# One plain feed-forward chunk instead of two, and two chunk pairs opened early

## Chip, cores, metric

The kernel runs on one core of a Trainium2 chip. The metric is the device time of one execution in microseconds (us): before the change a median of 2859.53 us over 3 runs (2858.35 to 2859.78). "Before" is the kernel as it was; line numbers L... are those of its profile unless said otherwise.

## What is computed

A trunk of two layers over 768 tokens (512 of one request, 256 of another), width 1024. Each layer is a feed-forward block, a mixer, and a second feed-forward block, so there are four feed-forward blocks, f0 to f3. The mixers (a gated linear recurrence between f0 and f1, windowed attention between f2 and f3) are not touched. What is:

```python
x = x + 0.5 * swiglu_ffn(rmsnorm(x, norm_g[li, 0]), ffn_w1[li, 0], ffn_w2[li, 0])

def swiglu_ffn(x, w1, w2):                    # D_FF = 2816
    gate, up = jnp.split(x @ w1, 2, axis=-1)
    return (jax.nn.silu(gate) * up) @ w2
```

The hidden width 2816 is 22 chunks of 128 columns; a chunk has 128 gate columns and 128 up columns.

## The kernel before

**Number format.** All products of float32 operands are made of three TensorE matmuls on "hi" and "lo" halves: hi·hi, hi·lo, lo·hi. Each operand is split once: ScalarE (ACT) casts it to hi, VectorE (DVE) subtracts to get lo (`split`, L265 to L267 for activations; L166/L167 and L199/L200 for weights).

**A plain chunk** (`up_plain`, L398) multiplies 8 blocks of input columns (k) by the gate and the up weights, for one half of the tokens (384) at a time: 2 × 8 × 3 = 48 matmuls of 384 columns per token half, 96 for both.

**A pair** (`up_pair`, L431) treats a chunk's gate and up weights as a 2 × 2 matrix product over (two halves of the input width) × (two halves of the tokens) and does it with 7 products instead of 8 (Strassen's scheme in Winograd's form): 7 × 4 × 3 = 84 matmuls of 384 columns. The products take these operands (`FACTOR`, L45): p1 takes b00 and p2 takes b10, the two input halves of token half 0; p3 takes b11; p4, p5, p6, p7 take t4, t1, t2, t3. The t's are differences of the b's of **both** token halves, formed by `sums`/`mix` (L348 to L362): four subtractions and four splits of 768 elements per partition, for each of two k-halves (kp 0 and 1), on DVE and ACT. One product is 12 matmuls, 6 for each kp; the first of each three needs only the hi parts.

**A feed-forward block** (`ffn`, L503): 5 groups of 4 chunks, each group followed by its share of the second matrix (`down_quad`, L458, matmuls at L479), and 2 last chunks. Chunks 0 and 1 (`PLAIN = 2`) are plain, and are worked token half by token half: chunk 0 half 0, chunk 1 half 0, chunk 0 half 1, chunk 1 half 1. Chunks 2 to 21 are pairs. While chunks 0 and 1 run for token half 0, the rest of the preparation of token half 1 is taken in at set points (`run_later`, L406): normalised token blocks (`norm_block`, L300; scaling L306) are transposed by TensorE (`turn`, L323), copied and split; then `sums` makes the t's. In f1 to f3 the sixth token block gets its norm only as the preceding stage ends.

**Weights.** `load_next` (L143) loads a chunk's gate and up weights into raw tiles (`wr`, 4 buffers) through SP's queue; GpSimd (POOL) adds one raw half into another by accumulating DMAs (L141) for a pair. A list of steps then turns raw tiles into split tiles (`w`, at most 8 units held at once, `WBUFS`); `ahead` (L244) takes the next step whenever a product has released its tile. For pairs these steps include two in-place sums on DVE (L206 after p1, L210 after p2). p5's lo part is made on POOL, the others on DVE (L200).

A scheduler in the framework orders the recorded instructions on each engine; each engine then executes its list strictly in order.

Of the kernel before, what the change touches and what calls it, by code (L numbers as in the profile page):

```python
# [12 lines left out]
AF = mybir.ActivationFunctionType  # L13
# [3 lines left out]
P = 128  # L17
# [28 lines left out]


class Trunk:
# [83 lines left out]
        self.nc.scalar.dma_start(self.band, self.consts[3])  # L132

    def plan(self, key, src, shape):
        self.queue.append((key, (src,), shape, None))

    def plan_quad(self, key, srcs, shape, order):
        self.queue.append((key, srcs, shape, order))

    def into(self, out, src):  # L140
        self.nc.gpsimd.dma_start(out, src, accum_op=ALU.add)  # L141

    def load_next(self):  # L143
        key, srcs, shape, how = self.queue.pop(0)
        raws = []
        for src in srcs:
            t = self.wp.tile([P, 1024], F32, tag="wr", name=self.name("wr"), bufs=RAWBUFS)
            raw = t[:, : shape[0] * shape[1]].rearrange("p (a b) -> p a b", a=shape[0])
            if len(srcs) < 4:
                src = src.rearrange("(k p) c -> p k c", p=P)  # L150
# [6 lines left out]
        self.loaded.append((len(raws), steps))  # L157

    def wtile(self):
        return self.wp.tile([P, 1024], F32R, tag="w", name=self.name("w"), bufs=WBUFS)  # L160
# [11 lines left out]
    def quad_steps(self, key, raws, srcs, order):  # L172
        nc = self.nc
        flat = lambda t: t.rearrange("p a b -> p (a b)")
        up = len(raws) == 2
        if up:
            a11, a12, a21, a22 = (flat(t[:, h : h + 4, :]) for t in raws for h in (0, 4))
            three = [srcs[1].rearrange("(k p) c -> p k c", p=P)[:, :4, :]]
        else:
            a11, a12, a21, a22 = (flat(t) for t in raws)  # L180
            three = [srcs[2][:, i : i + 1, :] for i in range(2)]
        s3 = []
        for i, src in enumerate(three):
            t = self.wp.tile([P, 512], F32, tag="s3", name=self.name("s3"), bufs=2)
            self.last_load = nc.sync.dma_start(t.rearrange("p (a b) -> p a b", a=src.shape[1]), src)
            self.into(t, a11[:, i * 512 : (i + 1) * 512])
            s3.append(t)
        self.into(a21, a22)

        def split(name, srcs, eng=None):  # L190
            if up:
                w = self.wtile()
                hi, lo = w[:, :512], w[:, 512:]
            else:
                hi, lo = self.wtile(), self.wtile()
            n = srcs[0].shape[-1]
            for i, src in enumerate(srcs):
                h, l = (t[:, i * n : (i + 1) * n] for t in (hi, lo))
                nc.scalar.copy(h, src)  # L199
                (eng or nc.vector).tensor_sub(l, src, h.bitcast(F32))  # L200
            view = lambda t: t.rearrange("p (a b) -> p a b", a=4 if up else 2)
            self.staged[(*key, name)] = (view(hi), view(lo), 1 if up else 2)

        def p1():
            split("p1", [a11])
            nc.vector.tensor_add(a11, a11, a21)  # L206
# [14 lines left out]
        return [(1 if up else 2, steps[name]) for name in order]  # L221

    def stage_next(self):
        if not self.loaded:
            self.load_next()
        steps = self.loaded[0][1]
        n, go = steps.pop(0)
        go()
        self.held += n
        if not steps:  # L230
            self.loaded.pop(0)
        while self.queue and sum(e[0] for e in self.loaded) + len(self.queue[0][1]) <= RAWBUFS:
            self.load_next()

    def take(self, key):
# [142 lines left out]
    def plan_ffn(self, tag, w1, w2):  # L378
        def up(i):
            gate, up = (w1[:, c * P : (c + 1) * P] for c in (i, NF + i))  # L380
            if i < PLAIN:
                self.plan((tag, i, 0), gate, (NC, P))
                self.plan((tag, i, 1), up, (NC, P))
            else:
                self.plan_quad((tag, i), (gate, up), (NC, P), UP)

        for g in range(GROUPS):
            for i in range(4 * g, 4 * g + 4):
                up(i)
# [8 lines left out]
    def up_plain(self, tag, j, half):  # L398
        pss = []
        for c in range(2):  # L400
            wh, wl = self.take((tag, j, c))
            ps = self.ps(H)
            for k in range(NC):
                b = self.operand(f"b{k // 4}{half}", k % 4)
                self.mm3(ps, (wh[:, k, :], wl[:, k, :]), b, k == 0, k == NC - 1)
                if half == 0 and k in (((), (2, 6)), ((3, 7), (3, 7)))[j][c]:  # L406
                    self.run_later()
            if half:
                self.done((tag, j, c))
# [18 lines left out]
                )  # L428
        self.done((*key, name))

    def up_pair(self, tag, j):  # L431
        nc = self.nc
        key = (tag, j)
        a, b, c, d = (self.ps(H) for _ in range(4))
        v, w, t = (self.tmp(H) for _ in range(3))
        p = lambda name, ps, first, last: self.product(key, name, FACTOR[name], ps, first, last)
        p("p1", a, True, False)
        nc.scalar.copy(v, a)
        p("p7", c, True, False)
        nc.scalar.copy(w, c)  # L440
        p("p2", a, False, True)
        nc.scalar.activation(a, a, AF.Silu)
        p("p5", d, True, False)
        nc.vector.tensor_sub(w, w, d)  # L444
        p("p4", c, False, True)
# [57 lines left out]
    def ffn(self, tag, next_row):  # L503
        for g in range(GROUPS):
# [7 lines left out]
            def gather(ts, kp):  # L512
                self.mix(ts[0], ts[1], ts[2], ts[3], lambda name, src: put(name, src, kp))

            if g == 0:
# [766 lines left out]
```

## Time and profile before

| | |
|---|---|
| runs shown | 2859.53 us median (2858.35 to 2859.78) |
| the profiled execution's own time | 2859.59 us |
| its span in the trace | 2857.8 us |
| TensorE busy | 2804.0 us (98%) |
| VectorE busy | 2175.1 us (76%) |
| ScalarE busy | 1317.9 us (46%) |
| mean granted TensorE clock | 0.997 |

The span is what the trace covers; the execution's own time is 1.8 us longer. A busy time is the union of the instructions' intervals on an engine. TensorE's matmuls overlap (each is shown with some 334 ns for 384 columns, and starts 173 ns after the one before), so lost time on TensorE is read from the "idle before" column and from distances between starts.

### The profile page before, as it was taken

The page shows a single profiled execution, that of the slowest core. Times are in us where ns is not written, and L with a number is a line of the kernel's source. Part 1 is how long each engine was busy: PE and PEld are TensorE (multiplying, and loading weights), DVE is VectorE, ACT ScalarE, POOL GpSimd, SP SyncE. Part 2 cuts the span into 40 slices and gives each one's busy share as a digit, 9 for nine tenths or more (in the row PEclk, how much of TensorE's full clock was granted, in tenths as well). Part 3 has the DMA queues.
Part 4 walks back from the last instruction along what each step waited for, and adds up shares of the span by engine and source line. Part 5 has one row for each costly group of instructions (what it writes and reads, how often), then busy time and mean ns, then how long its engine had stood idle before and what let it go on. Part 6 is the DMA issues. An engine that isn't in the chain of part 4 may idle for free. (4 is left out here: it accounts for less than half of the span.)

```text
span 2857.8 us, 40567 instructions
## 1 busy us (share of the span) xinstructions
PE 2804.0 (98%) x15225; PEld 2556.4 (89%) x15225; DVE 2175.1 (76%) x3750; ACT 1317.9 (46%) x2454; POOL 358.4 (13%) x402
## 2 busy tenths in 40 slices
PE   8999999999999999999999999999999999999998
PEld 8889999889899889998998998999887779989997
DVE  7788787477577658878878877887847868778877
ACT  7344443434344435434444543444457755434443
POOL 1111111000000001111111111111002211111110
PEclk9999999999999999999999999999999999999999
DMA  6554454311111133554444355444412113554443
GB/s 164 127 124 122 117 136 120 111 45 38 45 41 35 61 94 89 133 129 122 122 115 111 89 134 130 121 122 119 125 67 75 37 46 91 135 129 122 118 122 96
DMA packets 330102, 291.37 MB, mean 102 GB/s; under 512 B 11609, under 2 KB 257841, under 8 KB 329905
## 3 DMA queue, kind: packets, MB, share of 16 engines
q1 hardware_dynamic: 294064, 212.43, 25.2%
q0 software_dynamic: 31680, 62.93, 12.6%
q10 hardware_dynamic: 4160, 13.42, 1.3%
q8 instruction: 119, 1.95, 0.3%
q14 instruction: 79, 0.64, 0.1%
HBM read 216.39 MB, written 9.44 MB: 79 GB/s over the span
## 5 line engine op out<-in xcount | busy, mean ns | idle before, releaser
L421 PE MATMUL ps<-big,w 128*128 128x384 f32 x6720 | 1173.1, 334 | 3.1 <-DVE tA L444 3.0
L421 PEld LDWEIGHTS ps<-big,w 128*128 128x128 f32 x6720 | 1165.4, 188 | 9.0 <-DVE tA L444 7.3
L199 ACT CAST w<-wr 128x512 fp32r<-128x512 f32 x600 | 415.9, 707 | 722.6 <-PE ps L421 320.6
L479 PE MATMUL ps<-w,big 128*128 128x512 f32 x2520 | 586.5, 391 | 17.9 <-DVE x L501 17.8
L479 PEld LDWEIGHTS ps<-w,big 128*128 128x128 f32 x2520 | 469.6, 188 | 129.8 <-DVE x L501 17.4
L200 DVE TENSOR_TENSOR w<-wr,w 128x512 fp32r<-128x512 f32 (+1 forms) x520 | 438.9, 854 | 94.7 <-ACT w L199 86.1
L501 DVE SCALAR_TENSOR_TENSOR x<-ps,x 128x512 f32<-128x512 f32 x468 | 305.8, 683 | 20.8 <-PE ps L479 10.4
L141 POOL DMA_DIRECT2D s<-wr x120 | 105.6, 880 | 1333.9 <-DMA wr<-in_ffn_w_dram 590.5
L261 PE MATMUL ps<-w,big 128*128 128x512 f32 x624 | 249.9, 401 | 0.2
L263 PE MATMUL ps<-w,big 128*128 128x512 f32 x624 | 245.3, 393 | 1.3 <-DVE big L330 1.3
L262 PE MATMUL ps<-w,big 128*128 128x512 f32 x624 | 244.8, 392 | 0.0
L266 ACT CAST big<-tA 128x384 fp32r<-128x384 f32 x296 | 147.9, 512 | 175.6 <-DVE tA L449 72.4
L261 PE MATMUL ps<-big,w 128*128 128x384 f32 (+2 forms) x640 | 221.6, 347 | 2.1 <-ACT big L266 2.0
L262 PE MATMUL ps<-big,w 128*128 128x384 f32 (+2 forms) x640 | 217.4, 340 | 0.6 <-DVE big L267 0.5
L263 PE MATMUL ps<-big,w 128*128 128x384 f32 (+2 forms) x640 | 216.3, 338 | 0.0
L167 DVE TENSOR_TENSOR w<-wr,w 128x1024 fp32r<-128x1024 f32 x92 | 111.8, 1223 | 81.7 <-ACT w L166 57.7
L141 POOL DMA_DIRECT2D wr<-wr x100 | 87.2, 872 | 682.5 <-DVE tA L350 317.9
L267 DVE TENSOR_TENSOR big<-tA,big 128x384 fp32r<-128x384 f32 x296 | 164.2, 566 | 8.0 <-ACT big L266 4.6
L206 DVE TENSOR_TENSOR wr<-wr,wr 128x512 f32<-128x512 f32 (+1 forms) x100 | 79.4, 794 | 114.8 <-DMA wr<-wr 85.0
L166 ACT CAST w<-wr 128x1024 fp32r<-128x1024 f32 x92 | 96.6, 1052 | 122.2 <-PE ps L262 101.1
L263 PEld LDWEIGHTS ps<-w,big 128*128 128x128 f32 x624 | 117.7, 189 | 27.0 <-DVE big L330 2.0
L200 POOL TENSOR_TENSOR w<-wr,w 128x512 fp32r<-128x512 f32 x80 | 118.6, 1482 | 158.4 <-ACT w L199 145.3
(170 smaller groups left out, 3327.5 us busy)
## 6 DMA issues: line engine op xcount, KB each, us to landing
wr<-in_ffn_w_dram SPq DMA_DIRECT2D x264, 512.0 KB, 3.9
s<-in_ffn_w_dram SPq DMA_DIRECT2D x120, 256.0 KB, 3.0
s<-wr POOLq DMA_DIRECT2D x120, 256.0 KB, 3.8
wr<-wr POOLq DMA_DIRECT2D x80, 256.0 KB, 3.9
wr<-in_hg_w_in_dram SPq DMA_DIRECT2D x40, 512.0 KB, 3.8
wr<-wr POOLq DMA_DIRECT2D x20, 512.0 KB, 4.6
spill<-x ACTq DMA_DIRECT2D x12, 512.0 KB, 3.1
x<-spill ACTq DMA_DIRECT2D x12, 512.0 KB, 3.3
```

The costliest lines, as they stand in the source:

```text
L141: self.nc.gpsimd.dma_start(out, src, accum_op=ALU.add)
L167: self.nc.vector.tensor_sub(lo, raw, hi.bitcast(F32))
L199: nc.scalar.copy(h, src)
L200: (eng or nc.vector).tensor_sub(l, src, h.bitcast(F32))
L261: nc.tensor.matmul(out, a[0], b[0], start=first, stop=False)
L262: nc.tensor.matmul(out, a[0], b[1], start=False, stop=False)
L263: nc.tensor.matmul(out, a[1], b[0], start=False, stop=last)
L266: self.nc.scalar.copy(hi, src)
L267: self.nc.vector.tensor_sub(lo, src, hi.bitcast(F32))
L421: self.nc.tensor.matmul(ps, a[x], b[y], start=first and k == 0 and i == 0, stop=k == 3 and i == 2, skip_group_check=True,)
L479: nc.tensor.matmul(ps, a[x], w[y], start=name == chain and kp == 0 and q == 0, stop=kp == 1 and q == 2, skip_group_check=True,)
L501: self.nc.vector.scalar_tensor_tensor(x, ps, c, x, ALU.mult, ALU.add)
```

## The change

- `PLAIN = 1`: only chunk 0 is plain. Chunk 1 becomes a pair; the number of groups stays 5 and of last chunks 2.
- In each block the order becomes: chunk 0 half 0; then `open_pairs` does p1 of chunks 1 and 2 and p2 of chunks 1 and 2 (with the copy and the SiLU that follow them); then chunk 0 half 1; then the five other products of chunk 1, those of chunk 2, and chunk 3 as a whole pair. The points of `run_later` move with it: two within chunk 0, one behind each of the four opened products.
- The weights of chunks 1 and 2 are planned as one entry of four raw tiles; their steps come as p1, p1, p2, p2, then the rest of chunk 1, then of chunk 2 (`OPENED`).
- For the two opened pairs p5's lo part is made on DVE instead of POOL.

```diff
-PLAIN = 2
+PLAIN = 1
+EARLY = 2
 UP = ("p1", "p7", "p2", "p5", "p4", "p6", "p3")
+OPENED = ("p1", "p2", "p7", "p5", "p4", "p6", "p3")
...
     def load_next(self):
-        key, srcs, shape, how = self.queue.pop(0)
+        lists, count = [], 0
+        for part in self.queue.pop(0):
+            steps, n = self.load_part(*part)
+            lists.append(steps)
+            count += n
+        if len(lists) > 1:
+            opened = [steps.pop(0) for _ in range(EARLY) for steps in lists]
+            lists.insert(0, opened)
+        self.loaded.append((count, sum(lists, [])))
...
-            "p5": lambda: split("p5", [a21], nc.gpsimd if up else None),
+            "p5": lambda: split("p5", [a21], nc.gpsimd if order == UP else None),
...
+            elif i < PLAIN + 2:
+                two.append(((tag, i), (gate, up), (NC, P), OPENED))
+                if len(two) == 2:
+                    self.queue.append(two)
...
-                if half == 0 and k in (((), (2, 6)), ((3, 7), (3, 7)))[j][c]:
+                if half == 0 and k in ((), (2, 6))[c]:
                     self.run_later()
...
+    def open_pairs(self, tag, js):
+        nc = self.nc
+        opened = {j: (self.ps(H), self.tmp(H)) for j in js}
+        for j, (a, v) in opened.items():
+            self.product((tag, j), "p1", FACTOR["p1"], a, True, False)
+            nc.scalar.copy(v, a)
+            self.run_later()
+        for j, (a, _) in opened.items():
+            self.product((tag, j), "p2", FACTOR["p2"], a, False, True)
+            nc.scalar.activation(a, a, AF.Silu)
+            self.run_later()
+        return opened
...
-                ts = {}
-                for half in range(2):
-                    for j in range(PLAIN):
-                        t = ts[2 * j + half] = self.up_plain(tag, j, half)
-                        name = f"b{j}{half}"
-                        if name != "b01":
-                            put(name, t, 0)
-                gather(ts, 0)
+                plain = [self.up_plain(tag, 0, 0)]
+                put("b00", plain[0], 0)
+                opened = self.open_pairs(tag, range(PLAIN, PLAIN + EARLY))
                 self.run_later(len(self.deferred))
+                plain.append(self.up_plain(tag, 0, 1))
             for kp in range(2):
-                if g == 0 and kp == 0:
-                    continue
                 ts = []
                 for j in range(2):
-                    for half, t in enumerate(self.up_pair(tag, 4 * g + 2 * kp + j)):
+                    i = 4 * g + 2 * kp + j
+                    if i < PLAIN:
+                        ts += plain
+                        continue
+                    for half, t in enumerate(self.up_pair(tag, i, opened.get(i))):
```

**What it moves on the engines.** Compared row by row, the instruction lists of before and after differ only at the start and in the first group of each of the four blocks. The second block, f1, is shown. In the rows, `w` are split weights, `wr` raw weights, `ps` accumulators in PSUM, `big` activations; the line numbers of the changed kernel are a little higher (L200 is L212 there, L306 is L318, L421 is L438).

TensorE in f1 before, at the end of the plain chunks (L261 to L263 are their three matmuls; the last plain accumulator is ps_9343) and at the start of chunk 2, the first pair (L421): p1 (b00), p7 (t3: big_9180 for kp 0, big_9196 for kp 1), p2 (b10), p5 (t1: big_9172, big_9188):

```order
L261 MATMUL ps_9343<-big_9145,w_9001 128x384
L262 MATMUL ps_9343<-big_9145,w_9001 128x384
L263 MATMUL ps_9343<-big_9145,w_9002 128x384
L421 MATMUL ps_9397<-big_8978,w_9270 128x384 x6
L421 MATMUL ps_9397<-big_8981,w_9270 128x384 x6
L421 MATMUL ps_9399<-big_9180,w_9274 128x384 x6
L421 MATMUL ps_9399<-big_9196,w_9274 128x384 x6
L421 MATMUL ps_9397<-big_9041,w_9302 128x384 x6
L421 MATMUL ps_9397<-big_9044,w_9302 128x384 x6
L421 MATMUL ps_9400<-big_9172,w_9306 128x384 x6
L421 MATMUL ps_9400<-big_9188,w_9306 128x384 x6
```

TensorE at the same place after the change: the end of chunk 0 (L273 to L275) is followed at once by the products of chunk 1 that need the t's (t3: big_9206 for kp 0, big_9222 for kp 1; t1: big_9198, big_9214; t2: big_9209, big_9225; t4: big_9203, big_9219):

```order
L274 MATMUL ps_9307<-big_9164,w_8855 128x384
L275 MATMUL ps_9307<-big_9164,w_8856 128x384
L438 MATMUL ps_9342<-big_9206,w_9192 128x384 x6
L438 MATMUL ps_9343<-big_9198,w_9240 128x384 x6
L438 MATMUL ps_9343<-big_9214,w_9240 128x384 x5
L438 MATMUL ps_9342<-big_9222,w_9192 128x384
L438 MATMUL ps_9343<-big_9214,w_9240 128x384
L438 MATMUL ps_9341<-big_9209,w_9272 128x384 x6
L438 MATMUL ps_9342<-big_9222,w_9192 128x384 x5
L438 MATMUL ps_9341<-big_9225,w_9272 128x384 x4
L438 MATMUL ps_9342<-big_9203,w_9256 128x384 x6
```

The products that need no t have moved ahead of this place, so that the first use of a t follows the plain matmuls directly, and the scheduler has interleaved the products of kp 0 with each other.

VectorE in f1 before, from the split of the first operands of token half 0 on (big_8978), past the weights of chunk 1 (L167), to the norm of the sixth token block (L306, big_9014):

```order
L267 TENSOR_TENSOR big_8978<-big_8961,big_8978 128x2x384
L267 TENSOR_TENSOR big_8981<-big_8961,big_8981 128x2x384
L167 TENSOR_TENSOR w_8992<-wr_8742,w_8991 128x1024
L465 TENSOR_TENSOR x_8537<-x_8537,x_8543 128x512
L167 TENSOR_TENSOR w_9002<-wr_8754,w_9001 128x1024
L305 RECIPROCAL stat_9015<-stat_9015 128x1
L306 TENSOR_SCALAR big_9014<-x_8543,stat_9015 128x1024
```

VectorE at the same place after the change, from the second of these splits to the norm of the sixth token block (L318, big_9033):

```order
L279 TENSOR_TENSOR big_9000<-big_8980,big_9000 128x2x384
L212 TENSOR_TENSOR w_9010<-wr_8859,w_9010 128x512
L212 TENSOR_TENSOR w_9014<-wr_8867,w_9014 128x512
L218 TENSOR_TENSOR wr_8859<-wr_8859,wr_8861 128x512
L218 TENSOR_TENSOR wr_8867<-wr_8867,wr_8869 128x512
L212 TENSOR_TENSOR w_9024<-wr_8859,w_9024 128x512
L212 TENSOR_TENSOR w_9028<-wr_8867,w_9028 128x512
L222 TENSOR_TENSOR wr_8859<-wr_8859 128x512
L222 TENSOR_TENSOR wr_8867<-wr_8867 128x512
L317 RECIPROCAL stat_9034<-stat_9034 128x1
L279 TENSOR_TENSOR big_9060<-big_9043,big_9060 128x2x384
L318 TENSOR_SCALAR big_9033<-x_8558,stat_9034 128x1024
```

Eight weight instructions of 512 (four splits, four sums) and one activation split now stand ahead of that norm, where two weight splits of 1024 and one update of x stood; the update of x has moved behind it.

More of the change, by code (lines that the diff above doesn't have):

```diff
@@ L134, in plan, with plan_quad @@
     def plan(self, key, src, shape):
-        self.queue.append((key, (src,), shape, None))
-    def plan_quad(self, key, srcs, shape, order):
-        self.queue.append((key, srcs, shape, order))
+        self.queue.append([(key, (src,), shape, None)])
+    def plan_quad(self, *args):
+        self.queue.append([args])
     def into(self, out, src):
@@ L231, in stage_next @@
             self.loaded.pop(0)
-        while self.queue and sum(e[0] for e in self.loaded) + len(self.queue[0][1]) <= RAWBUFS:
+        while self.queue and sum(e[0] for e in self.loaded) + sum(len(p[1]) for p in self.queue[0]) <= RAWBUFS:
             self.load_next()
@@ L429, in product, with up_pair @@
         self.done((*key, name))
-    def up_pair(self, tag, j):
+    def open_pairs(self, tag, js):
[10 more added lines that the diff above has]
+        return opened
+    def up_pair(self, tag, j, opened=None):
         nc = self.nc
         key = (tag, j)
-        a, b, c, d = (self.ps(H) for _ in range(4))
-        v, w, t = (self.tmp(H) for _ in range(3))
+        a, v = opened or (self.ps(H), self.tmp(H))
+        b, c, d = (self.ps(H) for _ in range(3))
+        w, t = (self.tmp(H) for _ in range(2))
         p = lambda name, ps, first, last: self.product(key, name, FACTOR[name], ps, first, last)
-        p("p1", a, True, False)
-        nc.scalar.copy(v, a)
+        if not opened:
+            p("p1", a, True, False)
+            nc.scalar.copy(v, a)
         p("p7", c, True, False)
         nc.scalar.copy(w, c)
-        p("p2", a, False, True)
-        nc.scalar.activation(a, a, AF.Silu)
+        if not opened:
+            p("p2", a, False, True)
+            nc.scalar.activation(a, a, AF.Silu)
         p("p5", d, True, False)
```

5 lines of the change are left out of this document (4 added, 1 removed).

## The prediction

> **What bounds the kernel now.** The page's first part, then TensorE's waits (line that waited, what ended the wait, us in all, times, longest):
>
> ```profile
> span 2857.8 us, 40567 instructions
> PE 2804.0 (98%) x15225; PEld 2556.4 (89%) x15225; DVE 2175.1 (76%) x3750; ACT 1317.9 (46%) x2454; POOL 358.4 (13%) x402
> PE ps L479 <- DVE x L501: 17.8, 37, 0.6
> PE ps L421 <- DVE tA L444: 3.0, 8, 0.7
> PE ps L261 <- ACT big L266: 2.0, 1, 2.0
> PE ps L323 <- DVE big L306: 1.9, 2, 1.2
> ```
>
> TensorE is busy 98% of the span and waits nowhere for long, so its instruction count is the time: fewer matmuls shorten the kernel, unless new waits take the place. The waits above lie in the second products (L479), at a group's last pair (L444) and at the program's start. The change touches the starts of the four blocks, so next I read the engines' busy time in these four stretches, from the first plain matmul to the last (columns: length, then busy time and instruction count of PE, PEld, DVE, ACT, POOL, then clock and DMA):
>
> ```profile
> 14.33:55.58 41.25, 39.72 (x216) 38.65 (x217) 35.29 (x46) 32.74 (x54) 5.54 (x5) 0.92 0.52 127
> 1069.79:1106.40 36.61, 36.52 (x219) 35.87 (x218) 32.64 (x42) 26.84 (x45) 3.88 (x3) 1.00 0.21 52
> 1569.12:1605.80 36.68, 36.63 (x219) 35.99 (x218) 33.23 (x44) 26.79 (x45) 4.49 (x3) 1.00 0.22 53
> 2353.90:2390.71 36.81, 36.61 (x219) 35.86 (x218) 32.84 (x42) 27.01 (x45) 3.88 (x3) 1.00 0.22 52
> ```
>
> TensorE loses nothing there, but DVE is busy 32.6 of 36.6 us: it works nearly as long as TensorE in just the stretch that is to be shortened. That decides this case.
>
> **What the change removes.** In each block a plain chunk (96 matmuls) becomes a pair (84): 12 matmuls of 384 columns fewer. Their pitch, from TensorE's list in f1 (start, length, count; the next group's start ends it):
>
> ```profile
> 1106.42 29.28 PE L421 MATMUL ps<-big,w 128*128 128x384 f32 x168
> 1135.54 4.88 PE L479 MATMUL ps<-w,big 128*128 128x512 f32 x19
> ```
>
> (1135.54 − 1106.42) / 168 = 0.1733 us, so 12 matmuls are 2.08 us and four blocks 8.3 us. That is all there is to gain: 2859.6 − 8.3 = 2851.3 us. [...]
>
> The first use of a t comes sooner. In f1 it stood 12 matmuls behind 1106.42; now it follows the plain matmuls, 48 matmuls (8.3 us) before 1106.42. The work that makes the t's does not shrink.
>
> **First wait: the sixth token block.** DVE's list in f1 (start, length, op, count, idle before):
>
> ```profile
> 1069.60 1.82 DVE L267 TENSOR_TENSOR big<-big,big 128x768 fp32r<-128x768 f32 x2
> 1071.34 1.22 DVE L167 TENSOR_TENSOR w<-wr,w 128x1024 fp32r<-128x1024 f32 x1
> 1072.47 0.69 DVE L465 TENSOR_TENSOR x<-x,x 128x512 f32<-128x512 f32 x1
> 1073.07 1.22 DVE L167 TENSOR_TENSOR w<-wr,w 128x1024 fp32r<-128x1024 f32 x1
> 1074.21 0.16 DVE L305 RECIPROCAL stat<-stat 128x1 f32<-128x1 f32 x1
> 1074.40 0.75 DVE L306 TENSOR_SCALAR big<-x,stat 128x1024 f32<-128x1024 f32 x1
> ...
> 1079.21 1.83 DVE L267 TENSOR_TENSOR big<-big,big 128x768 fp32r<-128x768 f32 x2 [1.53 <-ACT big L266]
> 1082.60 1.83 DVE L267 TENSOR_TENSOR big<-big,big 128x768 fp32r<-128x768 f32 x2 [1.56 <-ACT big L266]
> ```
>
> By distances between starts a 512-wide op takes 0.60 us (1072.47 to 1073.07) and a 768-wide one 0.87. After the change, from 1069.60: two splits 1.74, eight weight instructions 8 × 0.60 = 4.80, the reciprocal 0.2, one more split 0.87, the norm 0.75: the sixth block is ready at 1077.96, where before it was at 1075.15. TensorE's side:
>
> ```profile
> 1074.01 0.93 PE L323 MATMUL ps<-ident_r,big 128*128 128x128 f32 x7
> 1074.69 0.42 PE L261 MATMUL ps<-big,w 128*128 128x384 f32 x1
> ...
> 1075.30 0.71 PE L323 MATMUL ps<-ident_r,big 128*128 128x128 f32 x5
> ```
>
> Its transposes began at 1075.30 without a wait. Their new place is 8 plain matmuls (1.39 us) and 4 transposes (0.68/7 = 0.10 each) later, 1077.08. So TensorE waits some **1.0 us**; f3 has the same rows, f2 about 0.8. Bounds: 0, if DVE gets to the weights before 1069.60, and 2.8 us, the whole delay of the norm. I take 1.0, f1's value. The eight instructions need weights that POOL's accumulating DMAs have finished; those loads start when chunk 0's raw tiles come free, as chunk 2's did before, so I put no DMA wait there.
>
> **Second wait: the t's.** The transposes end about 1.8 us later than before, and ACT, then DVE follow. The [1.53] and [1.56] above show that DVE itself waited for ACT at this place, so most of its added work fits in, and not all of the delay adds up. The sums' first and last rows before:
>
> ```profile
> 1084.34 0.95 DVE L350 TENSOR_TENSOR big<-big,big 128x768 f32<-128x768 f32 x1
> ...
> 1099.05 2.69 DVE L267 TENSOR_TENSOR big<-big,big 128x768 fp32r<-128x768 f32 x3
> ```
>
> After: sums from 1086.1 on. Up to the lo part of t3 for kp 1 stand 15 ops of 768 (13.0), 5 of 512 (3.0) and 2 of 384 (0.9): 1103.1. TensorE starts the t products at 1106.42 − 8.32 + 1.0 = 1099.1 and reaches the first matmul that needs this lo part 25 matmuls later, at 1103.4; t2's lo part comes 0.9 later (1104.0) and is needed 30 matmuls in (1104.3). So there is **no wait, with 0.3 us to spare**; bounds −0.3 (hidden) and +3, if the two DVE gaps of 1.5 us persist in full. p4 follows only 4 matmuls (0.7 us) behind p7's end, with ACT's copy between them (some 0.5 us and two semaphores): 0.2 us.
>
> **Third wait: the last pair of the group.** Chunk 3's raw tiles come free only when chunk 1's last weight is split (1101 by the same count), and those of the second products when chunk 3's are. Before:
>
> ```profile
> 1130.05 1.23 DVE L206 TENSOR_TENSOR wr<-wr,wr 128x1024 f32<-128x1024 f32 x1 [5.17 <-DMA wr<-wr]
> 1131.19 1.22 DVE L200 TENSOR_TENSOR w<-wr,w 128x1024 fp32r<-128x1024 f32 x1
> 1132.33 0.55 DVE L444 TENSOR_TENSOR tA<-tA,ps 128x384 f32<-128x384 f32 x1
> ```
>
> The sum at 1130.05 waits for the accumulating DMA, and L444, which TensorE's p3 needs, stands behind it; that is the wait of 3.0 us in 8 places quoted above. After, by my count of DVE's rows, the raw tiles come free 1.5 us later and L444's successor ends near 1133.0, where TensorE wants it at 1132.6: 0.4 us (bounds 0 and 0.7, the longest of those 8). POOL no longer makes p5's lo part for two chunks; DVE's two extra splits are in the counts.
>
> f1 to f3, each: −2.08 + 1.0 + 0.2 + 0.4 = about −0.5; f2's wait is 0.2 shorter: together −1.7.
>
> **The first block** has no late norm; the six token blocks come in from memory. Its sums:
>
> ```profile
> 35.75 1.83 DVE L267 TENSOR_TENSOR big<-big,big 128x768 fp32r<-128x768 f32 x2 [1.47 <-ACT big L266]
> 37.49 1.82 DVE L350 TENSOR_TENSOR big<-big,big 128x768 f32<-128x768 f32 x2
> ...
> 49.41 1.78 DVE L200 TENSOR_TENSOR w<-wr,w 128x512 fp32r<-128x512 f32 x1
> ...
> 51.72 2.68 DVE L267 TENSOR_TENSOR big<-big,big 128x768 fp32r<-128x768 f32 x3
> ...
> 55.60 4.67 PE L421 MATMUL ps<-big,w 128*128 128x384 f32 x26
> ```
>
> Ahead of L350 stand 10 weight ops (6.0) for two L167 (2.3): 3.7 us more, of which the 1.47 of idle takes part; the sums begin near 39.6 and end near 55.7, where before they ran from 37.49 to 54.4. TensorE arrives at 55.4 − 8.3 = 47.1, finds only kp 0's t's, and has some 30 matmuls to do before it needs kp 1's: I count 2.0 to 2.8 us of waits against the 2.08 removed and a wait of 0.6 at L444 that falls away. Taken: 0 (−2.7 to +2).
>
> **Sum.** 2859.6 − 1.7 + 0 = about **2858 us**, against this execution's own 2859.59 us (its span of 2857.8 and the 1.8 around it), which is 0.06 us above the median of the runs shown.
>
> **Rivals.**
> *The waits are covered.* If DVE runs ahead of my count, TensorE keeps its pace and gains the full 2.08 us a block: 2851.3 us. For it: no such wait before, and an order that the scheduler fitted to these dependencies. Against it: DVE's eight instructions ahead of the norm are in the list, and DVE has no idle time between 1069.60 and 1075. Chance 0.17.
> *The t's come late, and DVE becomes the bound.* Place: from the first L362 (L350's successor) to t3 of kp 1. I have 0.3 us to spare there; each us beyond is a us of TensorE. If the chain is 3 us later (both ACT gaps whole), a block loses 2.7 more, four blocks 10.8: 2868.8 us. From 2.2 us later per block on (1.9 × 4 = 7.6) the kernel is slower by over 0.2%. For it: DVE's 32.6 busy us of 36.6, in a stretch to be cut to 28.3, with 2.3 us of weight work added; one DVE split of 512 took 1.78 us, at 49.41. Against: ACT's order ahead of the sums is as before. Chance 0.30. Should its wait come in one piece, a further loss is possible: TensorE's first matmuls after the start stood 0.32 us apart instead of 0.173:
>
> ```profile
> 16.13 0.52 PE L261 MATMUL ps<-big,w 128*128 128x384 f32 x1
> 16.45 0.52 PE L262 MATMUL ps<-big,w 128*128 128x384 f32 x1
> ```
>
> [...]
> *The change saves no matmuls.* The lists show 48 fewer, so I give this 0.01, within "no change".
>
> **How the numbers follow.** Within 0.2% means within 5.7 us, about what a measurement of this kernel tells from no change: 2853.9 to 2865.3. The forecast holds 0.52, the covered waits 0.17, the late t's 0.30, the last 0.01. So faster 0.17, same 0.53, slower 0.30. The range goes down to 2852.5 (half of the first rival) and up to 2866.5, with about 0.2 left out.
>
> **What would show it.** In the trace after: 12 fewer 384-wide matmuls a block; a wait of about 1 us of the transposes (now L335) for the norm (L318) in f1, f2, f3 and none in f0; the first t product at about 1099 in f1; waits of L438 for splits (L279, L212) of 2 to 3 us in f0 and near 0 in the others; DVE without idle time through the block's start. I am wrong if the transposes do not wait (then 2851 to 2854), if L438 waits over 2 us for L279 in each block, or if a DMA holds up the sums in L218 at a block's start.

## The result, and the profile after

The changed kernel takes 2874.57 us (median of 6 runs, 2872.39 to 2876.84) where the kernel before takes 2858.94 us (6 runs, 2856.12 to 2859.78) beside it: a ratio of **1.0056 (95% interval 1.0045 to 1.0067)**, 15.6 us slower. The forecast was 2858.0 us with a range up to 2866.5. The profiled execution took 2872.39 us.

The line numbers below are those of the changed kernel, where not said otherwise: L273 to L275 are the plain matmuls, L438 the products of the pairs, L512 the second products, L279 and L212 the lo parts that DVE makes of activations and of weights, L278 and L211 ACT's hi parts, L163 the loads of raw weights, L143 the accumulating DMAs that POOL issues, L218 the sum a11 += a21 (L206 before), L222 the sum a12 += a11, L477 the subtraction w −= d (L444 before) and L480 to L488 the rest of a pair. In a pair a11 and a12 are the two input halves of the gate weights (one raw tile), a21 and a22 those of the up weights (another); the two accumulating DMAs make a21 += a22, and add a11 to a tile s, which holds a second load of the up weights' first half and serves p7.

The page's first part says of the changed kernel:

```profile
span 2870.6 us, 40607 instructions
PE 2801.7 (98%) x15177; PEld 2546.6 (89%) x15177; DVE 2194.9 (76%) x3802; ACT 1327.9 (46%) x2482; POOL 353.9 (12%) x406
```

TensorE has its 48 matmuls less (15177 against 15225) and is busy less, yet the span is 12.8 us longer: the time went into waits. TensorE's waits in the changed kernel (line that waited, what ended the wait, us in all, times, longest):

```profile
PE ps L438 <- DVE tA L477: 10.3, 10, 1.8
...
PE ps L274 <- DVE big L279: 4.2, 6, 1.9
PE ps L273 <- ACT big L278: 2.5, 3, 2.0
...
PE ps L335 <- DVE big L318: 1.8, 2, 1.1
```

The first row is the one to see: the wait for the subtraction that was 3.0 us before is now 10.3. The prediction looked for the new waits at the norm of the sixth token block and at the t's. For the norm (last row) there is none: that row was 1.9 us before, and both of its waits lie at the program's start and in f0. To place the waits I take for each block the time from its first plain matmul to its first second product (L512), less the same of before (71.09, 65.74, 65.79 and 65.94 us):

| Block | forecast | changed kernel |
|---|---|---|
| f0 | 0 | +4.29 |
| f1 | −0.5 | +2.38 |
| f2 | −0.7 | +3.52 |
| f3 | −0.5 | +3.35 |

Each length is that of the one profiled execution. The four make 13.5 us; the two executions differ by 12.8. So all of the loss lies in the first group of each block, and f0 and the others are to be read apart.

**Blocks f1 to f3.** TensorE's list in f1 (start, length, count, what ended the idle time before):

```profile
1073.32 0.60 PE L273 MATMUL ps<-big,w 128*128 128x384 f32 x2
...
1080.74 0.45 PE L274 MATMUL ps<-big,w 128*128 128x384 f32 x1 [0.56 <-DVE big L279]
...
1102.98 19.32 PE L438 MATMUL ps<-big,w 128*128 128x384 f32 x108
1123.80 14.86 PE L438 MATMUL ps<-big,w 128*128 128x384 f32 x84 [1.49 <-DVE tA L477]
1139.25 2.35 PE L438 MATMUL ps<-big,w 128*128 128x384 f32 x12 [0.59 <-DVE tA L477]
1141.44 0.86 PE L512 MATMUL ps<-w,big 128*128 128x512 f32 x3
```

The head, 1073.32 to 1102.98, is 29.66 us, against 36.63 − 8.32 = 28.31 without waits: 1.35 us lost, where the forecast had 1.0. The products run to 1123.80 with hardly a pause, though the t's are used from 1102.98 on. Then come two waits for L477, 1.49 and 0.59 us by these rows. The second stands at the last product of the group, the place that the prediction had priced; the first does not. What DVE did ahead of the first of them (its list in the same block):

```profile
1112.90 0.69 DVE L212 TENSOR_TENSOR w<-s,w 128x512 fp32r<-128x512 f32 x1
1116.43 0.69 DVE L218 TENSOR_TENSOR wr<-wr,wr 128x512 f32<-128x512 f32 x1 [2.85 <-issue]
1117.04 0.55 DVE L480 TENSOR_TENSOR tA<-tA,ps 128x384 f32<-128x384 f32 x1
...
1122.13 0.55 DVE L488 TENSOR_TENSOR tA<-tA,tA 128x384 f32<-128x384 f32 x1
1122.60 0.68 DVE L212 TENSOR_TENSOR w<-wr,w 128x512 fp32r<-128x512 f32 x1
1123.20 0.54 DVE L477 TENSOR_TENSOR tA<-tA,ps 128x384 f32<-128x384 f32 x1
```

DVE stood still for 2.85 us at the sum of chunk 3's weights, with the rest of chunk 1's pair (L480 to L488) and chunk 2's L477 behind it. The view calls the reason "issue", that is, nothing that it can name. The SP queue's and POOL's lists have it:

```profile
1101.90 4.15 SPq L163 DMA_DIRECT2D wr<-in_ffn_w_dram  x2
```

```profile
1110.22 0.86 POOL L143 DMA_DIRECT2D wr<-wr  x1 [2.77 <-ACT w L211]
```

Chunk 3's raw weights are asked for from 1101.90 on, when a raw tile comes free; the second of the two loads, with a21 and a22, landed at 1109.55; so the accumulating DMA that makes its a21 is issued at 1110.22. It landed at 1116.35, and L218 started 0.08 us later. In the kernel before, POOL had issued chunk 3's a21 at 1080.01 and DVE came to the sum 28.8 us after, with nothing to wait for:

```profile
1080.01 0.86 POOL L141 DMA_DIRECT2D wr<-wr  x1 [1.92 <-issue]
```

```profile
1108.84 0.69 DVE L206 TENSOR_TENSOR wr<-wr,wr 128x512 f32<-128x512 f32 x1
```

**Block f0.** DVE's list in the changed kernel (the two splits at 35.44 are those of b01, the ones at 40.05 those of b11; the plain chunk's second half reads b01 and then b11):

```profile
30.00 0.69 DVE L218 TENSOR_TENSOR wr<-wr,wr 128x512 f32<-128x512 f32 x1
33.62 0.69 DVE L218 TENSOR_TENSOR wr<-wr,wr 128x512 f32<-128x512 f32 x1 [2.94 <-DMA s<-wr]
...
35.44 1.82 DVE L279 TENSOR_TENSOR big<-big,big 128x768 fp32r<-128x768 f32 x2
...
40.05 1.82 DVE L279 TENSOR_TENSOR big<-big,big 128x768 fp32r<-128x768 f32 x2
```

Chunk 2's sum overwrites the a11 that its s accumulation still reads; POOL issued that DMA at 28.51 and it landed at 33.43. Everything behind it in the list comes late by it, and TensorE, which is through with b01 after 12 matmuls, waits 1.94 us for b11:

```profile
38.78 0.34 PE L273 MATMUL ps<-big,w 128*128 128x384 f32 x1
41.06 0.45 PE L274 MATMUL ps<-big,w 128*128 128x384 f32 x1 [1.94 <-DVE big L279]
41.34 3.73 PE L438 MATMUL ps<-big,w 128*128 128x384 f32 x12
```

Then 12 matmuls take 3.73 us. The granted clock says why (length, busy times and counts of PE, PEld, DVE, ACT, POOL, clock, DMA share, GB/s):

```profile
41.00:45.00 4.00, 3.94 (x14) 3.94 (x15) 4.00 (x7) 0.14 (x1) 0.00 (x0) 0.59 0.19 55
```

Before, the same four microseconds held 25 matmuls at a clock of 1.00. Behind this, f0 waits 1.0 us in two pieces for the t's (at 56.2 and 56.9) and 1.1 us for L477 at 71.5, again behind a chunk 3 sum that DVE waited 2.60 us for.

### The profile page after: what moved, and what is told of

The parts are those of the page before. It is cut to its first block, busy times and chain, and to the rows that moved or that the text cites. A ratio compares the mean times of both kernels' runs of the same rounds, so it can differ in the third digit from the quotient of the medians.

```text
span 2870.6 us, 40607 instructions
## 1 busy us (share of the span) xinstructions
PE 2801.7 (98%) x15177; PEld 2546.6 (89%) x15177; DVE 2194.9 (76%) x3802; ACT 1327.9 (46%) x2482; POOL 353.9 (12%) x406
## 3 DMA queue, kind: packets, MB, share of 16 engines
q8 instruction: 119, 1.95, 0.3%
## 4 chain that ended last, share of the span: by engine, by line
PE 62%; DVE 25%; DMA 6%; issue 4%; ACT 2%; POOL 1%; DVEq 0%; POOLq 0%; SPq 0%; ACTq 0%
PE ps L438 23%; PE ps L512 10%; PE ps L274 7%; PE ps L275 7%; PE ps L273 7%; DVE w L212 6%; DVE big L279 5%; PE ps L703 3%; DMA wr<-wr 3%; DVE x L534 3%; DMA wr<-in_ffn_w_dram 3%; DVE wr L222 1%; DVE tA L366 1%; PE ps L797 1%; POOL big L1170 1%
## 5 line engine op out<-in xcount | busy, mean ns | idle before, releaser
L438 PE MATMUL ps<-big,w 128*128 128x384 f32 x7056 | 1240.2, 335 | 11.5 <-DVE tA L477 10.3
L438 PEld LDWEIGHTS ps<-big,w 128*128 128x128 f32 x7056 | 1224.5, 188 | 24.0 <-DVE tA L477 16.7
L211 ACT CAST w<-wr 128x512 fp32r<-128x512 f32 (+1 forms) x624 | 429.9, 704 | 712.7 <-PE ps L438 302.6
L512 PE MATMUL ps<-w,big 128*128 128x512 f32 x2520 | 586.8, 391 | 18.8 <-DVE x L534 18.8
L512 PEld LDWEIGHTS ps<-w,big 128*128 128x128 f32 x2520 | 469.4, 188 | 131.1 <-ACT tA L487 17.7
L212 DVE TENSOR_TENSOR w<-wr,w 128x512 fp32r<-128x512 f32 (+1 forms) x548 | 452.9, 837 | 94.5 <-ACT w L211 86.0
L143 POOL DMA_DIRECT2D s<-wr x124 | 108.7, 877 | 1387.8 <-DMA wr<-in_ffn_w_dram 606.1
L273 PE MATMUL ps<-w,big 128*128 128x512 f32 x624 | 249.2, 399 | 0.2
L275 PE MATMUL ps<-w,big 128*128 128x512 f32 x624 | 244.6, 392 | 1.4 <-DVE big L342 1.3
L278 ACT CAST big<-tA 128x384 fp32r<-128x384 f32 x296 | 148.2, 513 | 201.2 <-DVE tA L482 87.5
L273 PE MATMUL ps<-big,w 128*128 128x256 f32 (+2 forms) x512 | 178.4, 350 | 2.7 <-ACT big L278 2.5
L143 POOL DMA_DIRECT2D wr<-wr x104 | 90.5, 870 | 718.0 <-DVE tA L362 313.0
L274 PE MATMUL ps<-big,w 128*128 128x256 f32 (+2 forms) x512 | 174.5, 342 | 4.3 <-DVE big L279 4.2
L275 PE MATMUL ps<-big,w 128*128 128x256 f32 (+2 forms) x512 | 173.1, 339 | 0.0
L218 DVE TENSOR_TENSOR wr<-wr,wr 128x512 f32<-128x512 f32 (+1 forms) x104 | 81.9, 790 | 119.0 <-DMA wr<-wr 81.7
L279 DVE TENSOR_TENSOR big<-tA,big 128x384 fp32r<-128x384 f32 x296 | 167.0, 575 | 5.9 <-ACT big L278 2.7
L179 DVE TENSOR_TENSOR w<-wr,w 128x1024 fp32r<-128x1024 f32 x84 | 102.2, 1223 | 81.7 <-ACT w L178 75.9
L178 ACT CAST w<-wr 128x1024 fp32r<-128x1024 f32 x84 | 88.2, 1052 | 122.3 <-PE ps L274 101.4
L275 PEld LDWEIGHTS ps<-w,big 128*128 128x128 f32 x624 | 117.2, 188 | 27.7 <-DVE big L342 2.0
L273 PEld LDWEIGHTS ps<-w,big 128*128 128x128 f32 x624 | 117.5, 188 | 22.1 <-ACT w L178 0.3
```

The source lines that it names most:

```text
L179: self.nc.vector.tensor_sub(lo, raw, hi.bitcast(F32))
L273: nc.tensor.matmul(out, a[0], b[0], start=first, stop=False)
L274: nc.tensor.matmul(out, a[0], b[1], start=False, stop=False)
L275: nc.tensor.matmul(out, a[1], b[0], start=False, stop=last)
L278: self.nc.scalar.copy(hi, src)
L279: self.nc.vector.tensor_sub(lo, src, hi.bitcast(F32))
```

## The experiments

Theory A: DMAs that land late stop DVE's in-order list at the sums, and TensorE waits for what stands behind them. Theory B: DVE has too much work in the shortened stretch, whatever stands first (the prediction's rival, the late t's, is its form). The expectations call the operand for which f0's second half waited b01; by the count of matmuls above it is b11, the next one. The table has the medians, the ratio to the kernel before on the same chip, and the difference per block formed as above, from one profiled execution of each kernel.

| Kernel | us | ratio, interval | f0 | f1 | f2 | f3 |
|---|---|---|---|---|---|---|
| sums late, pairs | 2861.83 | 1.0009, 1.0000 to 1.0019 | +3.85 | −1.07 | −0.57 | +0.88 |
| before, sums late, pairs | 2860.40 | 1.0003, 0.9993 to 1.0012 | +0.04 | +0.03 | 0.00 | −0.01 |
| p5 on POOL | 2883.53 | 1.0080, 1.0065 to 1.0095 | +10.17 | +2.65 | +3.11 | +4.38 |
| no opening | 2873.86 | 1.0049, 1.0034 to 1.0064 | +5.39 | +2.03 | +1.34 | +2.45 |
| sums turned | 2896.20 | 1.0136, 1.0120 to 1.0151 | +8.96 | +4.75 | +6.84 | +8.74 |
| before, sums turned | 2874.65 | 1.0063, 1.0050 to 1.0075 | +0.02 | +0.46 | +0.89 | +0.68 |
| sums turned, no opening | 2888.15 | 1.0107, 1.0093 to 1.0121 | +9.28 | +2.93 | +2.31 | +3.94 |
| all sums late | 2859.03 | 1.0007, 0.9999 to 1.0016 | +2.80 | −1.05 | −0.88 | −0.54 |
| all late, f0's behind b01 | 2855.93 | 0.9997, 0.9988 to 1.0005 | −1.01 | −1.00 | −0.49 | −1.17 |
| all late, f0 as before | 2854.92 | 0.9992, 0.9983 to 1.0001 | −1.33 | −1.07 | −0.81 | −1.17 |
| before, all sums late | 2858.21 | 1.0005, 0.9996 to 1.0014 | −1.12 | +0.01 | +0.01 | +0.01 |
| late from chunk 3 on | 2869.61 | 1.0038, 1.0025 to 1.0052 | +3.88 | +3.50 | +2.19 | +2.35 |

### The sums made late, and its control

```diff
         def p1():
             split("p1", [a11])
-            nc.vector.tensor_add(a11, a11, a21)
+            if not up:
+                nc.vector.tensor_add(a11, a11, a21)
...
+        def p6():
+            if up:
+                nc.vector.tensor_add(a11, a11, a21)
+            split("p6", [a11])
```

The second sum goes from p2 to p3 in the same way.

> The changed kernel with one edit: for the gate/up pairs the two sums on the raw weights (a11 += a21, a12 += a11), which stood right behind the splits p1 and p2, are made only in the steps p6 and p3 that need them. Theory A (an accumulating DMA that lands late stops DVE's in-order list at the sum, and what stands behind it, the split of b01 in the first block and the subtractions of chunks 2 and 3 at the groups' end, keeps TensorE waiting): the first block's DVE wait of 2.94 us for the s DMA and the TensorE waits of 10.3 us for the subtraction go for the most part, about 10 to 13 us, so 2861 to 2865 us. Theory B (DVE has too much work in the shortened stretch, whichever of its instructions comes first): 2871 to 2876 us.

> The kernel before with the same edit, as a control: before, TensorE waited 3.0 us in all for the subtraction behind the sum. Theory A: at most those 3 us are to be had, 2856 to 2860 us, so the edit by itself makes no kernel much faster. Theory B: no change, 2858 to 2860 us; if the edit gains 5 us or more here too, what it does in the changed kernel says nothing of the change.

Measured: 2861.83 us, 12.7 less than the changed kernel, and 2860.40 for the kernel before with the same edit, no gain, just above what was expected. Theory B falls for f1 to f3, since no DVE work was taken out. DVE's list in f1 of the changed kernel with late sums (L228 is the sum, L489 the subtraction, L493 and L496 further steps of chunk 1's pair):

```profile
1113.74 0.55 DVE L493 TENSOR_TENSOR tA<-ps,tA 128x384 f32<-128x384 f32 x1
1114.21 0.55 DVE L496 TENSOR_TENSOR tA<-tA,tA 128x384 f32<-128x384 f32 x1
...
1116.29 0.55 DVE L291 TENSOR_TENSOR big<-tA,big 128x384 fp32r<-128x384 f32 x1
1116.76 0.68 DVE L228 TENSOR_TENSOR wr<-wr,wr 128x512 f32<-128x512 f32 x1
...
1120.51 0.54 DVE L489 TENSOR_TENSOR tA<-tA,ps 128x384 f32<-128x384 f32 x1
```

Counted from the block's first plain matmul (1074.61 here, 1073.32 in the changed kernel), the sum starts after 42.2 us instead of 43.1, nearly as late as it did, and chunk 3's loads are asked for after 26.8 instead of 28.6. But chunk 1's pair now stands ahead of the sum, where it stood behind it, DVE waits for no DMA there, and L489 comes after 45.9 us instead of 49.9. For f0 the expectation was wrong: DVE still came to chunk 2's sum too early and waited 3.02 us, so f0 stayed at +3.85.

### POOL's help, and the opening left out

```diff
-            "p5": lambda: split("p5", [a21], nc.gpsimd if order == UP else None),
+            "p5": lambda: split("p5", [a21], nc.gpsimd if up else None),
```

> The changed kernel with one edit: the lo part of p5 is made on POOL for the two opened chunks too, as for all other pairs, which takes 8 subtractions of 512 elements (0.6 us each) off DVE in the four stretches. Theory A: DVE still waits for the DMAs at the same sums; 2872 to 2876 us. Theory B: each block gets 1.2 us of DVE time back, some 2 to 5 us in all: 2868 to 2872 us.

```diff
-            elif i < PLAIN + 2:
-                two.append(((tag, i), (gate, up), (NC, P), OPENED))
-                if len(two) == 2:
-                    self.queue.append(two)
...
-                opened = self.open_pairs(tag, range(PLAIN, PLAIN + EARLY))
```

> The changed kernel with one plain chunk, but without the opening: the products p1 and p2 of chunks 1 and 2 stand where they stand in every other group, behind the second token half. The late t's (the rival of the prediction, not opened): the t products start 48 matmuls (8.3 us) sooner than in the changed kernel, while the t's come no sooner, so TensorE waits some 5 to 9 us in each block: 2890 to 2905 us. Theory A alone, if the t's were in time anyway: 2872 to 2880 us.

With p5 on POOL both theories missed: the kernel took 2883.53 us, 9 more than the changed kernel instead of the same or 2 to 5 less, 6 of them in f0. It is no test of B's price, because the edit brought a wait of its own: one of the two subtractions moved to POOL in each block took 21.04 us in f0 and 6.8 to 7.1 us in f1 to f3 (more on this below), where it stands ahead of chunk 3's accumulating DMA in POOL's list. Without the opening the kernel took 2873.86 us, the same as with it: the number that theory A gave, and 16 us less than the least that the late t's would have cost. TensorE's waits in f1 (1076 to 1142 us) of that kernel (L434 is the product, L466 ACT's copy behind p7):

```profile
PE ps L335 <- DVE big L318: 1.2, 1, 1.2
PE ps L434 <- ACT tA L466: 1.1, 1, 1.1
```

The t's cost 0.2 us there. So the late t's, which I had priced at 5 to 9 us a block without the opening, are not what bounds these blocks. But neither row is a wait behind a sum, so in f1 of this kernel theory A has the number and not the place. As for the opening, the products put between the two halves bought nothing measurable by themselves.

### The sums turned round

```diff
-                nc.vector.tensor_add(a11, a11, a21)
-            split("p6", [a11])
+                nc.vector.tensor_add(a21, a21, a11)
+            split("p6", [a21 if up else a11])
```

(in the kernel with late sums, with a12 += a21 for the other one)

> The changed kernel with the sums of the gate/up pairs made late, as in the first experiment, and the other way round: a21 += a11 and a12 += a21 instead of a11 += a21 and a12 += a11, so that no sum overwrites the a11 that the accumulating s DMA still reads. Theory A: the first block's DVE wait of 3.0 us for the s DMA goes, the split of b01 comes 3 to 4 us sooner, TensorE's wait of 2.0 us there and part of the waits for the t's (2.4 us) go; 3 to 5 us less than the late sums alone, 2857 to 2859 us. Theory B (DVE is out of time in the first block anyway): 2861 to 2863 us.

> The kernel before with the same late and turned sums, as a control. Theory A: nothing there waits for the s DMA; 2857 to 2861 us, so one plain chunk against two stand within 0.1% of each other once the sums wait for no DMA. Theory B: the same.

> The changed kernel with the late and turned sums and without the opening. Theory A with the t's in time: as with the opening, 2857 to 2861 us. If the opened products are what covers the t's: 2 to 4 us in each block more than with the opening, 2866 to 2874 us.

All three expectations failed by far: 2896.20, 2874.65 and 2888.15 us. The wait in f0's second half did go, as A said (no wait of 0.3 us or more stands between 30 and 47 us), but it was repaid many times. The edit keeps the tile with a21 and a22 in use until p3; in the other direction it is free when p4 and the sum are done. The SP queue's list in f0 with turned sums:

```profile
57.00 1.70 SPq L163 DMA_DIRECT2D wr<-in_ffn_w_dram  x2
...
63.85 1.43 SPq L163 DMA_DIRECT2D wr<-in_ffn_w_dram  x2
```

Chunk 3's raw tiles were asked for from 48.87 on with the late sums alone, now from 57.00. TensorE's waits in this kernel (L450 the products, L489 the subtraction, L484 ACT's copy):

```profile
PE ps L450 <- DVE tA L489: 19.1, 21, 3.3
...
PE ps L450 <- ACT tA L484: 7.7, 3, 4.3
```

It was not what I meant to test, but it suggests that the path from a free raw tile over the load and the accumulating DMA to the sum has no slack: held longer, the tiles cost the kernel before 17 us too (2874.65 against 2857.83), most of it outside the blocks' first groups, which lose under 1 us each.

### All sums late, and f0 taken apart

The kernel with all sums late has them in p6 and p3 for the second products' weights too. On it stand two further kernels. One puts chunk 1's and 2's sums in f0 behind the split of b01 in DVE's list:

```diff
         def p6():
-            nc.vector.tensor_add(a11, a11, a21)
+            with self.tc.issue_after(self.b01) if key in (("f0", 1), ("f0", 2)) else nullcontext():
+                nc.vector.tensor_add(a11, a11, a21)
```

(self.b01 is the last DVE instruction of that split). The other gives f0 its two plain chunks back and leaves f1 to f3 as changed:

```diff
+        plain = 2 if tag == "f0" else PLAIN
...
-            if g == 0:
+            if g == 0 and tag == "f0":
...
+                    for j in range(2):
+                        t = ts[2 * j + half] = self.up_plain(tag, j, half)
...
+            elif g == 0:
```

> The changed kernel with the two sums made late in their own direction (a11 += a21 in step p6, a12 += a11 in step p3) for the gate/up pairs, as in the first experiment, and for the second products' weights too. Theory A: with the pairs alone 6.0 us of TensorE's waits for the subtraction were left, one of 1.7 us behind the sum on the second products' weights; 1 to 4 us of them go: 2858 to 2861 us. If DVE's amount of work sets those waits: 2861 to 2863 us.

> The kernel with all sums late, and in the first block the sums of chunks 1 and 2 put behind the split of b01 in DVE's list, so that the wait for the s DMA comes behind it. Theory A: TensorE's wait of 2.0 us for b01 goes and the t's come no later; 2 to 3 us less than with the late sums alone. Theory B holds in the first block (DVE has no time left there, the t's come late whatever stands first): the wait moves from b01 to the t's, within 1 us of the late sums alone.

> The kernel with all sums late, and the first block as before the change (two plain chunks, nothing opened); the other three blocks with one plain chunk and two opened pairs. The first block lost 3.9 us with late sums against before; that goes: 4 to 5 us less than with the late sums alone, 2853 to 2858 us, at or a little below the kernel before.

> The kernel before with all sums late, as a control. Both theories: 0 to 3 us less than the kernel before (its waits for the subtraction were 3.0 us), 2855 to 2860 us.

All four times lie in or beside what theory A gave: 2859.03, 2855.93 (3.1 less than with all sums late, where A had 2 to 3), 2854.92 and 2858.21 us. The last, the control, was to be 0 to 3 us below the kernel before and is 1.1 above it by the medians, not told apart from no change. In f0 the place of two sums in the list is worth 3.8 us (+2.80 to −1.01). DVE's list with the sums behind b01 (L224 the sums, L286 the splits; b01's are those at 31.49):

```profile
31.49 1.83 DVE L286 TENSOR_TENSOR big<-big,big 128x768 fp32r<-128x768 f32 x2 [0.77 <-ACT big L285]
...
34.91 1.28 DVE L224 TENSOR_TENSOR wr<-wr,wr 128x512 f32<-128x512 f32 x2
```

With all sums late and no such order the second sum started at 33.31, after 2.94 us of waiting for the s DMA; here both run one behind the other from 34.91, 1.6 us after that, and wait for nothing, the split of b11 starts at 36.72 instead of 39.14, TensorE does not wait for it, and the sums for the t's begin 2.4 us sooner (39.06 instead of 41.48). So what B says of f0 is not so: DVE had that time, and lost it at the DMA. TensorE's wait for the subtraction in this kernel:

```profile
PE ps L447 <- DVE tA L486: 2.1, 5, 0.6
```

That is 10.3 us become 2.1. The best of them, with f0 as before, is 0.9992 of the kernel before with an interval that reaches 1.0001: 2 us less by the medians, not told apart from no gain.

### Late from chunk 3 on

```diff
-            if not up:
+            if order != UP:
...
-            if up:
+            if order == UP:
```

(four places in the kernel with late sums for the pairs: the opened chunks have their early sums back)

> The changed kernel with the sums late only for the pairs that are not opened (chunk 3 and all later ones); the opened chunks 1 and 2 keep a11 += a21 behind p1 and a12 += a11 behind p2. Theory A: the waits for the subtraction in blocks f1, f2 and f3 (2.4, 3.0 and 3.4 us there), which stand behind chunk 3's sum, go for the most part; the first block keeps its loss. 5 to 8 us less than the changed kernel, 2866 to 2870 us. If it is the sums of the opened chunks that cost: 2872 to 2876 us.

Measured 2869.61 us, 5.0 less than the changed kernel, at the upper end of what A gave. But f1 did not gain (+3.50 against +2.38). TensorE's waits in this kernel (L484 is ACT's copy behind p7):

```profile
PE ps L450 <- ACT tA L484: 4.0, 3, 2.0
PE ps L450 <- DVE tA L489: 2.8, 6, 1.2
```

The wait for the subtraction went for the most part, and one for ACT took its place. In f1 it is 1.95 us long, and the matmuls behind it lose time too:

```profile
1120.87 9.46 PE L450 MATMUL ps<-big,w 128*128 128x384 f32 x44 [1.95 <-ACT tA L484]
```

At 0.173 us these 44 matmuls would take 7.8; the granted clock was 0.57 in their first 4 us. DVE's list in f1 has the cause:

```profile
1117.80 0.69 DVE L228 TENSOR_TENSOR wr<-wr,wr 128x512 f32<-128x512 f32 x1 [2.98 <-issue]
1118.41 0.55 DVE L493 TENSOR_TENSOR tA<-ps,tA 128x384 f32<-128x384 f32 x1
```

Chunk 3's sum was late in the code but still ahead of chunk 1's pair (L493 to L494) in the list, ACT's split of that pair's result waited for DVE, and the copy stood behind it. So it is the sum's place in the list that counts, and what the scheduler makes of an edit has to be read from the list. Why it placed the sum there in this kernel and not in the first one was not tried.

## Why the prediction was wrong

**The gain of 2.08 us a block** was right: 48 matmuls fewer, at 0.173 us.

**First wait (the sixth token block, 1.0 us; its own rows give 1077.96 − 1077.08 = 0.88):** near in size, 1.35 us in f1 and by the same count 1.5 in f2 and 1.2 in f3, but wrong in place: TensorE did not wait for the norm, but for the split of b10 (0.56 of it above), which stands behind the eight weight instructions too, and ahead of the norm (L318):

```profile
1079.75 0.94 DVE L279 TENSOR_TENSOR big<-big,big 128x768 fp32r<-128x768 f32 x1
1080.61 0.75 DVE L318 TENSOR_SCALAR big<-x,stat 128x1024 f32<-128x1024 f32 x1
```

The next transposes start at 1081.90, when the norm is done.

**Second wait (the t's, none):** right, some 0.3 us in f1. So my main rival, the late t's at 2868.8 us, came nearest to the time by a mechanism that did not occur.

**Third wait (the last pair of the group, 0.4 us, at most 0.7): this step failed.** It measured 2.1 us between the rows in f1, and by the matmuls' distances 2.4, 3.0 and 3.4 us in f1, f2 and f3. Of these 0.75, 1.00 and 1.50 stand where I had priced them, behind the sum of the second products' weights, and 1.66, 1.95 and 1.92 behind chunk 3's own sum, for which the prediction has no term. I had read that chunk 3's raw tiles come free at about 1101 (1101.90 in the trace), and followed the delay only to the second products' weights behind them, from the 5.17 us row of before. In the kernel before, the DMA of chunk 3's sum was issued 28.8 us ahead of it, and that head start is what the change used up: chunks 1 and 2 now hold the four raw tiles. DVE's list was held by the instruction that waited (2.85 us at L218 in f1), and I had not named what stands behind this one.

**"I put no DMA wait there" failed in f0.** I asked when the weights arrive that DVE reads, not who still reads the ones that it overwrites. The wait of 2.94 us at L218 is for a reader. I had named a DMA that holds up L218 at a block's start as what would prove me wrong, and gave it no term.

**The first block, 0 (−2.7 to +2):** +4.29. Against the gain of 2.08 stand 2.1 us at b11, 1.5 at the lower clock of 0.59 (12 matmuls in 3.73 us; with all sums late 12 take 2.25), 1.0 for the t's (I had counted 2.0 to 2.8) and 1.1 at L477: 5.7 of the 6.4 us; the rest is in small pieces. For a slower rate the prediction has only the 0.32 us between TensorE's first matmuls, as a possible further loss, and no term.

**What is left of the forecast:** with the sums out of the way the runs agree with it. The kernel with all late sums and f0's behind b01 is 2.3 us below the kernel before with late sums (2855.93 against 2858.21; the intervals overlap), where I had −1.7 for the change; f1 to f3 gain 1.0, 0.5 and 1.2 us against it, where I had 0.5 to 0.7, and f0 comes out even (−1.01 against −1.12), where I had 0. So nothing speaks against the terms for DVE's and TensorE's work, though a gain of 2 us is not shown at this noise; the missing terms were DMA waits at the sums. That theory A's waits are the cause is shown by moving the sums alone; that chunk 3's load would be in time with a fifth and sixth raw tile was not tried.

## What to carry to other kernels

When a change packs more prefetched work into the same few staging tiles, follow each DMA that starts when one comes free to the first instruction of an in-order engine that needs it, and price what stands behind that instruction, not the instruction (in f1, L480 to L488 and L477 behind a wait of 2.85 us). For an update in place, ask who still reads the old value: in f0 DVE waited 2.94 us for a DMA that reads, about as long as the 2.85 us in f1 for one that writes. Put such updates into the list at their first use, and then read the list: code order and list order are not the same.

## What the runs showed of the hardware

**The clock does not go by the length of a wait alone.** After TensorE waits of 1.94 us (changed kernel), 2.04 us (without the opening), 3.28 and 4.29 us (turned sums) and 9.55 us (p5 on POOL), matmuls of 384 columns ran 0.32 us apart for some 2.5 to 4.5 us. After waits of 1.87 and 2.28 us (without the opening), 1.92 us (all sums late), 2.00 us (sums late in the pairs) and 2.33 us (turned sums) they kept 0.173. With all sums late:

```profile
40.14 0.44 PE L280 MATMUL ps<-big,w 128*128 128x384 f32 x1 [1.92 <-DVE big L285]
40.42 2.25 PE L444 MATMUL ps<-big,w 128*128 128x384 f32 x12
```

One wait in the first mixer, 1.74 us for ACT, stands in every kernel. In 5 of the 14 profiled executions the granted clock stayed at 1.00 in the 4 us behind it, in the other 9 it was 0.60 to 0.76. Here are its rows in the kernel before (clock 1.00) and in the one with all sums late (0.60):

```profile
587.49 2.26 PE L671 MATMUL ps<-big,big 128*128 128x128 f32 x12 [1.74 <-ACT big L696]
```

```profile
590.88 2.63 PE L709 MATMUL ps<-big,big 128*128 128x128 f32 x12 [1.74 <-ACT big L734]
```

What decides for waits of 1.7 to 2.4 us stays open.

**A subtraction on POOL took 21.04 us** in f0 with p5 on POOL; the 76 such subtractions in the changed kernel take 1.43 us on average. The rows of POOL and, in a second view, of TensorE:

```profile
37.80 21.04 POOL L212 TENSOR_TENSOR w<-wr,w 128x512 fp32r<-128x512 f32 x1 [8.13 <-ACT w L211]
```

```profile
58.90 3.57 PE L438 MATMUL ps<-big,w 128*128 128x384 f32 x10 [9.55 <-POOL w L212]
```

DVE ran from before its start to 58.2 us without a pause of 0.15 us or more, and its own splits kept their length (0.68 us for 512 elements). Up to 57.64 each of these instructions reads two operands from SBUF; the first that reads one from PSUM (ps) is

```profile
57.64 0.55 DVE L430 TENSOR_TENSOR tA<-tA,ps 128x384 f32<-128x384 f32 x1
```

The subtraction ended 1.20 us after the start of that row. The three of 6.8 to 7.1 us in f1 to f3 ended 1.23 us after the start of their first such L430, and there the DVE split behind L430 took 1.31 us instead of 0.68. The trace names no cause for these lengths. It shows that in f0 the subtraction stayed in its one row of 21.04 us while some 25 DVE instructions with two SBUF operands ran, and that in all four blocks it ended 1.20 or 1.23 us after the start of DVE's first instruction with a PSUM operand. Whether DVE's operands are the cause was not tried.
